# Two RMSNorm statistics moved from matmuls to GpSimd and a round trip through memory

## The chip, the cores and the metric

One core of a Trainium2 chip runs the whole program in one launch. The metric is the device time in microseconds (us) of that launch; of several runs the median is given. The core has a matrix engine (PE, TensorE, with a separate loader PEld for the stationary operand), a vector engine (DVE), an activation engine (ACT), a general engine (POOL, GpSimd) and an engine that only issues transfers (SP). On-chip memory has 128 lanes; a matmul sums over the lanes and writes to an accumulator bank, which DVE and ACT read. Each engine works off its own instructions in the order written, and waits on semaphores for those of others.

## The reference

The input is one sequence of 1024 positions with 1024 features, in float32. Two layers follow each other; each is a token mixer and a feed-forward block (FFN), both with a residual and an RMSNorm ahead. Layer 0 mixes with a short gated convolution, layer 1 with dilated attention in three branches.

```python
def rms_norm(x, g):
    y = x * lax.rsqrt(jnp.mean(x * x, axis=-1, keepdims=True) + EPS)
    return y * g

def short_conv_mixer(h, w_in, conv_k, w_out):
    b, c, u = jnp.split(h @ w_in, 3, axis=-1)
    y = depthwise_causal_conv(c * u, conv_k)          # 3 taps
    return (b * y) @ w_out

for i in range(DEPTH):                                # DEPTH = 2
    h = rms_norm(x, mix_norm[i])
    x = x + (short_conv_mixer(h, ...) if i % 2 == 0 else dilated_attention_mixer(h, ...))
    h = rms_norm(x, ffn_norm[i])
    x = x + (silu(h @ w_gate) * (h @ w_up)) @ w_down
return rms_norm(x, final_norm)
```

There are five norms: one ahead of each of the two mixers, one ahead of each of the two FFNs, and the final one. The change concerns the two ahead of the mixers.

## The kernel before

**Tiles.** Activations are kept transposed: the residual is eight tiles X of 128 features (lanes) by 1024 positions. So a sum over features, which a norm needs for each position, is a sum over the eight tiles and then over the 128 lanes. Every float32 product is made from three matmuls of a faster format: both operands are split into a high part (a copy rounded by ACT) and a low part (the difference, by DVE), and high x high, high x low and low x high are added in the bank. For weights the split is L142 (ACT) and L143 (DVE), and the weights come in by SP's loads (`load_raw`, L156, tile `raw`); sums of weights are made by DVE at L190 (tile `combo`).

**Products.** The large products are cut by Strassen's and Winograd's scheme into seven smaller products for each unit u; class `Strassen` has them in one list of pairs (u, m), and `mm` (L561 to L563) issues the three matmuls for each of four stationary tiles. After each product L567 (ACT) or L571 (DVE) takes the bank away. A list position n stands for time in this code: `start(n)` is called ahead of the n-th product, and a table of hooks says what is issued right after a certain product. So the order of work on each engine is written out by hand; nothing else decides it. The class `Conv` (layer 0) and its subclass `QueryKey` (layer 1, queries and keys) are such products. The list begins, by n: 0 (0,1), 1 (1,1), 2 (0,2), 3 (1,2), 4 (2,1), 5 (2,2), 6 (3,1), ..., 10 (0,6), 12 (0,7), 17 (1,4), 18 (2,6), 19 (0,3), 22 (2,5).

**The norm.** The products do not wait for the norm. The gain is put on the operand (L871 and L872 in the convolution; L903, L906, L907, L553, L554 for the operands that are differences), and 1/rms, which is one number for each position, is put on the results, much later: in the convolution at L969 and L959, in `QueryKey` at L1129 and L1131, and on the value tiles at L1508. Two forms are wanted: `rstd`, 128 x 1024, the same number in each lane, and `r`, 128 x 8, one number for each position in a lane. `Norm.stats` (L464 to L488) makes both from `acc`, the 128 x 1024 sum of squares over the eight tiles: eight matmuls with a column of ones sum over the lanes and leave the 1024 sums as 128 x 8 (L471, 16 instructions in the profile); ACT takes the square root (L474) and DVE the reciprocal (L475), which is `r`; DVE multiplies it with an identity into two diagonal tiles (L480); two matmuls of ones with these spread it over the lanes (L487, 4 instructions), and ACT copies the bank to `rstd` (L488). The convolution then squares `rstd` into `acc` (L1097).

In the convolution the squares (ACT, L885) are added up by accumulating transfers on GpSimd's queue (L886) into two tiles: `acc` for tiles 0 to 3, `upper` (named acc2 in the trace) for tiles 4 to 7. DVE adds the two at n = 18 (L1087); the sums over the lanes follow after product (0,3), n = 19, and the spreading after (2,5), n = 22. In `QueryKey` DVE adds the squares as each tile of X is finished (L424), the sums follow after (1,2), n = 3, and the spreading after (3,1), n = 6. The FFN norms use the same `Norm.stats`.

**Buffers and queues.** Tiles of 128 x 1024 come from a pool of 41 pages, and halves of them; a page is free when the last instruction that reads or writes it is done, so that an instruction can wait for a page that another tile had. SP's queue issues the weight loads, GpSimd's queue the stores, the accumulating transfers and the small round trips of the attention. There the attention already reduces over the lanes on GpSimd (`partition_all_reduce`, maximum, L1614) and inverts its denominators by way of memory (L1665 store, L1668 thin load, L1670 reciprocal, L1671 store, L1674 load to all lanes).

Of the kernel before, what the change touches and what calls it, by code (L numbers as in the profile page):

```python
# [98 lines left out]
def trunk(ctx: ExitStack, tc: tile.TileContext, x, gains_in, cwi, ck, cwo, wqkv, wo, relb,  # L99
# [295 lines left out]
    class Norm:  # L395
# [38 lines left out]
        def chained(self, k, c0, c1, late):  # L434


            s = slice(c0, c1)
            if self.acc is None:
                self.acc, self.rstd = page("acc"), page("rstd")
            acc = self.acc[:, s]  # L440
            if k == 1:
                self.odd = half_page("acc2")
            to = half_page("sq") if k > 1 else self.odd if k else acc
            nc.scalar.activation(to, X[k][:, s], AF.Square)
            add = lambda t: nc.vector.tensor_tensor(out=acc, in0=acc, in1=t, op=ALU.add)
            if k in (2, 3):
                nc.gpsimd.dma_start(out=(acc, self.odd)[k % 2], in_=to, accum_op=ALU.add)
            if k > 3:
                self.flush()
                self.put_off = lambda: add(to)  # L450
            if k == KT - 2:
                add(self.odd)
                self.odd = None
            if not late or k < 4:
                return
            if k == 4:
                self.rest, self.put_off = to, None
            elif k < KT - 1:
                add = lambda t: nc.vector.tensor_tensor(out=self.rest, in0=self.rest, in1=t, op=ALU.add)
            else:  # L460
                add(self.rest)
                self.rest = None

        def stats(self, c0, c1):  # L464

# [393 lines left out]
    class Conv(Strassen):  # L859
# [182 lines left out]
        def mix(self, group1):  # L1042
            norm = self.norm
            prep = self.operands()
            stats = norm.stats(0, S)

            def start(n):
                if n == 0:
# [27 lines left out]
                    next(prep)  # L1076
                elif n in (10, 12):
                    next(prep)
                elif n == 11:
                    next(prep)  # L1080
                    self.first(3)
# [1 line left out]
                    self.first(4)  # L1083
                elif n == 14:
                    next(prep, None)
                elif n == 18:
                    nc.vector.tensor_tensor(out=norm.acc, in0=norm.acc, in1=self.upper, op=ALU.add)  # L1087
                    del self.upper
                elif n == 20:
                    self.ahead = 3  # L1090

            def gather():
                next(stats)

            def spread():
                run(stats)
                nc.scalar.activation(norm.acc, norm.rstd, AF.Square)  # L1097
                self.ready = True

# [1 line left out]
            ensure(self.at(0, 1))  # L1101
            next(prep)
            ensure(self.at(0, 2))
            self.run(start, {(0, 3): gather, (2, 5): spread})
            group1("co", self.plain, self.hid)


# [3 lines left out]
    class QueryKey(Conv):  # L1111
# [43 lines left out]
        def mix(self):  # L1155
            norm = self.norm
            prep = self.differences()
            stats = norm.stats(0, S)
            x12 = []

            def start(n):
# [8 lines left out]
                elif n == 4:  # L1170
                    self.first(1)
                    ensure(self.at(4, 2))
                elif n == 5:
                    ensure(self.at(0, 6))
                elif n == 6:
                    ensure(self.at(1, 6))
# [8 lines left out]
                elif n in (10, 12):  # L1185
                    next(prep)
                elif n == 11:
                    next(prep)
                    self.first(3)
                elif n == 13:  # L1190
# [2 lines left out]
                    next(prep, None)  # L1193
                elif n == 20:
                    self.ahead = 3

            def gather():
                next(stats)

            def spread():  # L1200
                run(stats)
                self.ready = True

            def load():
                for k in range(4):
# [9 lines left out]
                start(n)  # L1215
                self.idle(n)

            norm.flush()
            self.base = op_state[1]
            ensure(self.at(0, 2))  # L1220
            self.products(filled, {(1, 2): gather, (3, 1): spread, (5, 1): load, (5, 7): last_operand})
            self.h = [[self.b[1 + 7 * h * (k < 4) + (1 + h) * (k > 3)][k % 4] for k in range(KT)] for h in range(2)]
            self.step(len(self.waiting) + 1)

# [844 lines left out]
```

## Time and profile before

| what | value |
|---|---|
| runs | 2140.90, 2142.98, 2143.33 us; median 2142.98 |
| profiled execution | 2143.59 us, its span 2141.5 us |
| PE busy | 2108.1 us (98% of the span) |
| DVE busy | 1744.0 us (81%) |
| ACT busy | 1007.4 us (47%) |
| POOL busy | 254.2 us (12%) |
| memory traffic | 212.48 MB read, 83.05 MB written, mean 138 GB/s |

How to read it: times are in us from the start of the span. A row of a timeline gives the start, the duration, the engine, the line of the kernel, the operation and its tiles (out<-in, shapes, number of instructions), and in brackets how long the engine had been idle before it and what ended that idle time. A row of the chain of waits gives start, duration and the instruction to which the end of the run is traced back. Matmuls overlap, so the row of one shows 0.39 us where they come 0.23 us apart. A line with "min/median/max" gives durations, or the time from a transfer's issue to its landing.

### The profile page before, as it was taken

Reading aid. Unit: us, or ns where it says so; the run is one execution under the profiler, and the core shown is the slowest. Engines: PE = TensorE matmul, PEld = TensorE weight load, DVE = VectorE, ACT = ScalarE, POOL = GpSimd, SP = SyncE. Lnnn points to the kernel's source line nnn. Section 1 sums busy time; section 2 is a strip of 40 time slices with the busy share of each in tenths; the row PEclk is TensorE's granted clock in tenths of the full one; section 3 lists DMA queues with packets and bytes.
Section 4 is the critical chain, followed back from the end, with each engine's and each line's share of the span. In section 5 each row is a group of like instructions: output and inputs, shape, how many; then the busy total and the mean of one; then the engine's idle time right before and its main releaser. Section 6 shows DMA issues by size and latency. Waiting matters only on the chain.

```text
span 2141.5 us, 31004 instructions
## 1 busy us (share of the span) xinstructions
PE 2108.1 (98%) x11086; PEld 1807.9 (84%) x11086; DVE 1744.0 (81%) x3272; ACT 1007.4 (47%) x1848; POOL 254.2 (12%) x370
## 2 busy tenths in 40 slices
PE   9999999999999999999999999899999999999998
PEld 7788878888888888877899989888788888888887
DVE  8798769988888888868967687777998888888876
ACT  7333426444444564335545544545543434356435
POOL 1000000110101000000323333221010101001000
PEclk9999999999999999999999999999999999999999
DMA  7322642233332576340767678755223333368432
GB/s 218 93 94 69 226 133 75 103 102 106 113 109 99 173 218 194 112 161 33 263 206 182 180 193 226 212 179 163 69 93 102 107 109 106 106 201 240 156 94 79
DMA packets 143354, 304.90 MB, mean 142 GB/s; under 512 B 48943, under 2 KB 55327, under 8 KB 143201
## 3 DMA queue, kind: packets, MB, share of 16 engines
q1 hardware_dynamic: 107488, 201.94, 31.3%
q0 software_dynamic: 28080, 86.29, 12.7%
q10 hardware_dynamic: 7632, 14.70, 1.8%
q8 instruction: 88, 1.44, 0.3%
q14 instruction: 66, 0.53, 0.1%
HBM read 212.48 MB, written 83.05 MB: 138 GB/s over the span
## 4 chain that ended last, share of the span: by engine, by line
PE 82%; DVE 7%; issue 3%; ACT 2%; DMA 2%; POOL 1%; SPq 0%; DVEq 0%; POOLq 0%; ACTq 0%
PE bank L563 19%; PE bank L561 19%; PE bank L562 19%; PE bank L371 4%; PE bank L372 4%; PE bank L370 4%; PE bank L653 3%; PE bank L656 3%; PE bank L655 3%; PE bank L1633 2%; POOL mb L1614 1%; PE bank L1503 1%; PE bank L1504 1%; PE bank L1505 1%; DVE w L143 1%
## 5 line engine op out<-in xcount | busy, mean ns | idle before, releaser
L563 PE MATMUL bank<-b,w 128*128 128x512 f32 x1952 | 761.7, 390 | 5.5 <-DVE w L143 5.3
L561 PE MATMUL bank<-b,w 128*128 128x512 f32 x1952 | 763.3, 391 | 2.1 <-ACT w L142 1.7
L562 PE MATMUL bank<-b,w 128*128 128x512 f32 x1952 | 761.1, 390 | 0.6 <-DVE b L872 0.6
L563 PEld LDWEIGHTS bank<-b,w 128*128 128x128 f32 x1952 | 366.8, 188 | 86.4 <-DVE w L143 10.2
L561 PEld LDWEIGHTS bank<-b,w 128*128 128x128 f32 x1952 | 367.0, 188 | 78.7 <-ACT w L142 2.8
L562 PEld LDWEIGHTS bank<-b,w 128*128 128x128 f32 x1952 | 366.9, 188 | 77.0 <-DVE b L872 1.8
L142 ACT ACTIVATE w<-combo 128x512 fp32r<-128x512 f32 (+2 forms) x488 | 249.2, 540 | 232.0 <-DVE combo L190 215.1
L143 DVE TENSOR_TENSOR w<-combo,w 128x512 fp32r<-128x512 f32 (+2 forms) x488 | 276.2, 579 | 39.4 <-ACT w L142 38.7
L567 ACT ACTIVATE part<-bank 128x512 f32<-128x512 f32 x186 | 110.7, 596 | 390.2 <-PE bank L563 388.5
L143 DVE TENSOR_TENSOR w<-raw,w 128x512 fp32r<-128x512 f32 (+2 forms) x342 | 189.5, 575 | 38.7 <-ACT w L142 38.7
L571 DVE TENSOR_TENSOR part<-part,bank 128x256 f32<-128x256 f32 (+1 forms) x366 | 170.5, 495 | 31.2 <-PE bank L563 16.7
L142 ACT ACTIVATE w<-raw 128x512 fp32r<-128x512 f32 (+2 forms) x342 | 166.7, 530 | 45.0 <-PE bank L563 12.2
L370 PE MATMUL bank<-w_hi,w 128*128 128x512 f32 (+1 forms) x400 | 153.8, 385 | 5.0 <-ACT w_hi L142 4.9
L371 PE MATMUL bank<-w_lo,w 128*128 128x512 f32 (+1 forms) x400 | 150.5, 376 | 1.2 <-DVE w_lo L143 1.2
L372 PE MATMUL bank<-w_hi,w 128*128 128x512 f32 (+1 forms) x400 | 150.1, 375 | 0.7 <-DVE w L143 0.7
L791 DVE TENSOR_TENSOR x<-x,bank 128x512 f32<-128x512 f32 x136 | 92.5, 680 | 29.1 <-PE bank L563 29.0
L492 DVE TENSOR_TENSOR x<-x,bank 128x512 f32<-128x512 f32 (+1 forms) x104 | 66.3, 642 | 59.6 <-PE bank L372 59.0
L190 DVE TENSOR_TENSOR combo<-raw 128x512 f32<-128x512 f32 (+1 forms) x172 | 111.1, 646 | 0.0
L370 PEld LDWEIGHTS bank<-w_hi,w 128*128 128x128 f32 x400 | 76.2, 191 | 18.8 <-ACT w_hi L142 5.4
L371 PEld LDWEIGHTS bank<-w_lo,w 128*128 128x128 f32 x400 | 76.0, 190 | 15.0 <-DVE w_lo L143 2.0
L372 PEld LDWEIGHTS bank<-w_hi,w 128*128 128x128 f32 x400 | 76.0, 190 | 14.5 <-DVE w L143 1.1
L554 DVE TENSOR_TENSOR b<-hin,b 128x512 fp32r<-128x512 f32 x126 | 79.4, 683 | 9.4 <-ACT b L553 9.4
(247 smaller groups left out, 3486.0 us busy)
## 6 DMA issues: line engine op xcount, KB each, us to landing
hin<-part SPq DMA_DIRECT2D x126, 256.0 KB
raw<-in_ffn_w_gate SPq DMA_DIRECT2D x44, 512.0 KB
raw<-in_ffn_w_up SPq DMA_DIRECT2D x44, 512.0 KB
part<-sum POOLq DMA_DIRECT2D x72, 256.0 KB, 2.3
raw<-in_ffn_w_down SPq DMA_DIRECT2D x48, 384.0 KB
raw<-in_attn_w_qkv SPq DMA_DIRECT2D x27, 512.0 KB
raw<-in_conv_w_in SPq DMA_DIRECT2D x24, 512.0 KB
part<-part POOLq DMA_DIRECT2D x36, 256.0 KB, 2.5
```

What stands on the lines that cost most here:

```text
L142: nc.scalar.activation(hi, src, AF.Copy)
L143: eng.tensor_tensor(out=lo, in0=src, in1=hi, op=ALU.subtract)
L190: eng.tensor_tensor(out=c, in0=a, in1=b, op=op)
L370: nc.tensor.matmul(b, whi[:, a], ahi[:, s], start=first, stop=False)
L371: nc.tensor.matmul(b, whi[:, a], alo[:, s], start=False, stop=False)
L372: nc.tensor.matmul(b, wlo[:, a], ahi[:, s], start=False, stop=last)
L561: nc.tensor.matmul(b, hi[:, a], bhi, start=start and k == 0, stop=False, skip_group_check=True)
L562: nc.tensor.matmul(b, hi[:, a], blo, start=False, stop=False, skip_group_check=True)
L563: nc.tensor.matmul(b, lo[:, a], bhi, start=False, stop=k == n - 1, skip_group_check=True)
L567: nc.scalar.activation(t, b, AF.Copy)
L571: nc.vector.tensor_tensor(out=t, in0=t, in1=b, op=ALU.add)
L791: nc.vector.tensor_tensor(out=X[n][:, half(h)], in0=X[n][:, half(h)], in1=b, op=ALU.add)
```

## The change

The statistics of the two mixer norms are made by a new generator, `Norm.aside`, in place of `Norm.stats`. It reduces `acc` over the lanes on GpSimd, which leaves the sum in every lane; lane 0 is stored to a small tile in memory and loaded back as 128 x 8; ACT takes the square root and DVE the reciprocal there; the result is stored to the same place, loaded to all 128 lanes as `rstd`, and loaded once more as `r`. The generator stops once (`yield`) between the thin load and the square root.

In the convolution the addition of the two accumulators becomes an accumulating transfer on GpSimd's queue at n = 10; the first part of `aside` is issued at n = 12, the second at n = 17; the squaring of `rstd` stays after (2,5). In `QueryKey` the first part is issued ahead of all products, the second at n = 5, and the flag `ready`, which lets results be taken away, is set at n = 11 in place of after (3,1). The code that GpSimd needs for its reductions is loaded ahead of the first of them, so that is now in the convolution and no longer in the attention. The FFN norms and the final norm are as before.

```diff
@@ -461,6 +461,23 @@
                 add(self.rest)
                 self.rest = None
 
+        def aside(self):
+
+            self.flush()
+            total, rd = page("total"), dram.tile([1, S], F32, name=f"rms{self.g}")
+            nc.gpsimd.partition_all_reduce(total, self.acc, 128, bass_isa.ReduceOp.add)
+            thin = consts.tile([128, KT], F32, name="thin", tag="thin", bufs=2)
+            rows = bass.AP(rd.tensor, rd.offset, [[KT, 128], [1, KT]])
+            nc.gpsimd.dma_start(rd, total[0:1])
+            nc.gpsimd.dma_start(thin, rows)
+            yield
+            nc.scalar.activation(thin, thin, AF.Sqrt, scale=1.0 / D, bias=eps)
+            nc.vector.reciprocal(thin, thin)
+            nc.gpsimd.dma_start(rows, thin)
+            nc.gpsimd.dma_start(self.rstd, bass.AP(rd.tensor, rd.offset, [[0, 128], [1, S]]))
+            r = self.r = consts.tile([128, KT], F32, name="r", tag="r", bufs=2)
+            nc.gpsimd.dma_start(r, bass.AP(rd.tensor, rd.offset, [[1, 128], [128, KT]]))
+
         def stats(self, c0, c1):
 
             self.flush()
@@ -1042,7 +1059,7 @@
         def mix(self, group1):
             norm = self.norm
             prep = self.operands()
-            stats = norm.stats(0, S)
+            stats = norm.aside()
 
             def start(n):
                 if n == 0:
@@ -1076,6 +1093,10 @@
                     next(prep)
                 elif n in (10, 12):
                     next(prep)
+                    if n == 10:
+                        nc.gpsimd.dma_start(out=norm.acc, in_=self.upper, accum_op=ALU.add)
+                    else:
+                        next(stats)
                 elif n == 11:
                     next(prep)
                     self.first(3)
@@ -1083,17 +1104,12 @@
                     self.first(4)
                 elif n == 14:
                     next(prep, None)
-                elif n == 18:
-                    nc.vector.tensor_tensor(out=norm.acc, in0=norm.acc, in1=self.upper, op=ALU.add)
-                    del self.upper
+                elif n == 17:
+                    run(stats)
                 elif n == 20:
                     self.ahead = 3
 
-            def gather():
-                next(stats)
-
             def spread():
-                run(stats)
                 nc.scalar.activation(norm.acc, norm.rstd, AF.Square)
                 self.ready = True
 
@@ -1101,7 +1117,7 @@
             ensure(self.at(0, 1))
             next(prep)
             ensure(self.at(0, 2))
-            self.run(start, {(0, 3): gather, (2, 5): spread})
+            self.run(start, {(2, 5): spread})
             group1("co", self.plain, self.hid)
 
 
@@ -1155,7 +1171,7 @@
         def mix(self):
             norm = self.norm
             prep = self.differences()
-            stats = norm.stats(0, S)
+            stats = norm.aside()
             x12 = []
 
             def start(n):
@@ -1171,6 +1187,7 @@
                     self.first(1)
                     ensure(self.at(4, 2))
                 elif n == 5:
+                    run(stats)
                     ensure(self.at(0, 6))
                 elif n == 6:
                     ensure(self.at(1, 6))
@@ -1185,6 +1202,7 @@
                 elif n in (10, 12):
                     next(prep)
                 elif n == 11:
+                    self.ready = True
                     next(prep)
                     self.first(3)
                 elif n == 13:
@@ -1194,13 +1212,6 @@
                 elif n == 20:
                     self.ahead = 3
 
-            def gather():
-                next(stats)
-
-            def spread():
-                run(stats)
-                self.ready = True
-
             def load():
                 for k in range(4):
                     x12.append(half_page("x12"))
@@ -1215,10 +1226,10 @@
                 start(n)
                 self.idle(n)
 
-            norm.flush()
             self.base = op_state[1]
+            next(stats)
             ensure(self.at(0, 2))
-            self.products(filled, {(1, 2): gather, (3, 1): spread, (5, 1): load, (5, 7): last_operand})
+            self.products(filled, {(5, 1): load, (5, 7): last_operand})
             self.h = [[self.b[1 + 7 * h * (k < 4) + (1 + h) * (k > 3)][k % 4] for k in range(KT)] for h in range(2)]
             self.step(len(self.waiting) + 1)
```

## The prediction

> **What bounds the kernel now.** Times below are of the one profiled execution, 2143.59 us (span 2141.5); it stands 0.61 us above the median of the runs, 2142.98, and I take the 0.61 off at the end. I read the page first: busy time, and the chain that ended last.
>
> ```profile
> PE 2108.1 (98%) x11086; PEld 1807.9 (84%) x11086; DVE 1744.0 (81%) x3272; ACT 1007.4 (47%) x1848; POOL 254.2 (12%) x370
> PE 82%; DVE 7%; issue 3%; ACT 2%; DMA 2%; POOL 1%; SPq 0%; DVEq 0%; POOLq 0%; ACTq 0%
> ```
>
> TensorE carries the time. So work taken from PE shortens the run one for one, unless PE then waits; work taken from DVE, ACT or POOL counts only where PE waits for it. Second, the chain in order of time, in the two stages that change: are the norm's own matmuls on it?
>
> ```profile
> 68.92 1.68 PE bank L471 x16
> 78.94 1.72 PE bank L487 x4
> 984.20 1.68 PE bank L471 x16
> 994.22 1.72 PE bank L487 x4
> ```
>
> All four groups are on it. The rows give start and time: the sums over the lanes and the spreading cost 3.40 us in each of the two norms, 6.80 in all.
>
> **The change part by part.**
> *Removed from PE.* Those four groups, 6.80 us. No matmul is added. The two FFN norms keep theirs.
>
> *Removed from DVE and ACT.* The addition of the two accumulators L1087, two L480 a norm, two copies L488 a norm. At zero: DVE and ACT follow PE there (rows below: ACT waits 3.70 us for PE at 66.24, DVE 2.75 for ACT at 82.42). They become idle time.
>
> *Added on GpSimd.* One all-reduce a norm and the round trip: a 4 KB store, a thin load, a thin store, a load to all lanes, a thin load of r. GpSimd's 12% leaves room; its queue holds nothing urgent beside them. What counts is whom the all-reduce disturbs and who waits for the trip. The attention stage has both already:
>
> ```profile
> L1614 POOL PARTITION_ALL_REDUCE mb<-m x16: 3180/3220/4057, 1125.0 to 1427.0; - x16
> 1299.27 3.18 POOL L1614 PARTITION_ALL_REDUCE mb<-m  x1
> 1299.88 1.78 DVE L1137 TENSOR_TENSOR kq_lo<-kq,kq_hi 128x512 fp32r<-128x512 f32 x1 [0.70 <-ACT kq_hi L1134]
> 1240.82 0.68 DVE L1137 TENSOR_TENSOR kq_lo<-kq,kq_hi 128x512 fp32r<-128x512 f32 x1
> 1236.80 3.22 POOL L1614 PARTITION_ALL_REDUCE mb<-m  x1 [5.32 <-issue]
> 1237.43 3.47 DVE L143 TENSOR_TENSOR w_lo<-raw,w_hi 128x1024 fp32r<-128x1024 f32 x2
> ```
>
> The same L1137 takes 0.68 us alone and 1.78 when it begins 0.61 after an all-reduce: without the hold it would have begun at 1299.88 + 1.78 - 0.68 = 1300.98, 1.71 after the all-reduce. The pair of L143 beside the other all-reduce takes 3.47, where a pair without a hold takes 2 x 1.2 (L424 of the same size: 1.23, below). So DVE, with two operands in memory, stands still until 1.7 us into an all-reduce.
> The Trainium skill's page "SBUF — State Buffer", section "Who interferes with whom", says that a DVE instruction with two SBUF inputs contends with a GpSimd instruction that reads SBUF, and that the second to issue is blocked for the whole instruction. The trace agrees on who is held, but not on how long: 1.7 of 3.2 us; the page's length is a rival below.
>
> *The hold in the attention norm.* The last addition to acc ends at 976.17, so the all-reduce begins near 976.4, beside this:
>
> ```profile
> 974.94 1.23 DVE L424 TENSOR_TENSOR acc<-acc,sq 128x1024 f32<-128x1024 f32 x1
> 976.08 0.68 DVE L143 TENSOR_TENSOR w<-raw,w 128x512 fp32r<-128x512 f32 x1
> 976.69 0.74 DVE L906 SCALAR_TENSOR_TENSOR t<-x,gains,t 128x512 f32<-128x512 f32 x1
> ...
> 978.91 0.75 DVE L907 SCALAR_TENSOR_TENSOR t<-x,gains,t 128x512 f32<-128x512 f32 x1
> 979.70 0.63 ACT L553 ACTIVATE b<-t 128x512 fp32r<-128x512 f32 x1 [0.82 <-DVE t L907]
> 980.24 1.66 ACT L142 ACTIVATE w<-raw 128x512 fp32r<-128x512 f32 x3
> 980.90 0.50 PE L561 MATMUL bank<-b,w 128*128 128x512 f32 x1 [0.63 <-ACT w L142]
> 990.47 0.62 ACT L142 ACTIVATE w<-raw 128x512 fp32r<-128x512 f32 x1
> ```
>
> DVE runs without a gap from L424 to the last L907, ACT's L553 waits for that, L142 stands behind L553, and PE waits for L142, already 0.63 us. L906 reads two operands from memory. Started at 976.4 the all-reduce holds it until 978.1, 1.4 later than now; if L143, which is running, delays the all-reduce first, until 978.5, 1.8 later. I take the middle, 1.65, all of it on PE's path. A loss of nothing (the all-reduce later than this chain) is the other end.
>
> *The trip in the attention norm.* From 976.4: 3.2 for the reduction, 3.1 for the store and 2.8 to 6.0 for the thin load (rows below) give 985.5 to 988.7; the square root now stands behind L142 of 990.47. At zero; were it later, that L142's successors would wait, and PE for them, one for one.
>
> *The convolution: the accumulator first.* The two accumulators are added by a DMA in place of DVE. It goes behind the six accumulations of L886:
>
> ```profile
> DMA to landing us min/median/max: 4.5/4.9/5.6
> 48.03 31.26 SPq L156 DMA_DIRECT2D raw<-in_conv_w_in  x7
> 49.28 2.56 ACT L871 ACTIVATE b<-x,gains 128x512 fp32r<-128x512 f32 x4
> 53.00 2.73 DVE L872 SCALAR_TENSOR_TENSOR b<-x,gains,b 128x512 fp32r<-128x512 f32 x4
> 58.12 0.69 DVE L190 TENSOR_TENSOR combo<-combo,raw 128x512 f32<-128x512 f32 x1 [1.79 <-DMA raw<-in_conv_w_in]
> 59.46 0.79 PE L563 MATMUL bank<-b,w 128*128 128x512 f32 x1 [2.35 <-DVE w L143]
> 60.05 0.63 PE L561 MATMUL bank<-b,w 128*128 128x512 f32 x1
> ...
> 62.84 0.39 PE L562 MATMUL bank<-b,w 128*128 128x512 f32 x1
> 63.07 0.39 PE L563 MATMUL bank<-b,w 128*128 128x512 f32 x1
> ```
>
> The first raw load of SP at 48.03 waited for the last accumulation (it took its page), so that landed by then. The new one issues there and lands 4.5 to 5.6 later, 52.5 to 53.6; the raw load that is now free to go some 5 us earlier shares the DMA engines, and I allow 55. The page of the second accumulator is now taken by one of the four operands made at 49.28 by ACT L871, so the last three of these, and the L872 of DVE behind them, start at 53 to 55 rather than follow on. Three L871 at 0.64, then one L872, two L190 and one L143 at 0.69: PE's operand comes at 55 + 1.9 + 4 x 0.69 = 59.7 at the late end, against 59.41 now; at the early end DVE's 1.79 us wait for the raw load hides it. The all-reduce then falls on the same DVE instructions and holds them 1.7: early it is hidden by the 1.79, late it adds all. Between a loss of nothing and 2.4 us I take 1.2.
>
> *The convolution: the trip.* GpSimd's code for the reduction is now loaded here; before the first attention reduction, where it was loaded until now, GpSimd sat idle for 6.34 us, so that is the most it can take:
>
> ```profile
> 1124.99 3.22 POOL L1614 PARTITION_ALL_REDUCE mb<-m  x1 [6.34 <-DMA ka<-kq]
> 1172.05 0.56 POOL L1665 DMA_DIRECT2D zdram<-z  x1 [5.17 <-ACT z L1656]
> 1175.16 0.59 POOL L1668 DMA_DIRECT2D zc<-zdram  x1 [2.55 <-DMA zdram<-z]
> DMA to landing us min/median/max: 2.8/5.9/6.3
> DMA to landing us min/median/max: 2.8/6.0/7.1
> 66.24 0.60 ACT L567 ACTIVATE part<-bank 128x512 f32<-128x512 f32 x1 [3.70 <-PE bank L563]
> 82.42 0.69 DVE L969 TENSOR_TENSOR part<-part,acc 128x512 f32<-128x512 f32 x1 [2.75 <-ACT acc L1097]
> ```
>
> The load starts behind the accumulation's issue, near 49, and is done by 55.3, beside the landing. So the reduction begins at 53.3 to 55.3 and ends at 56.5 to 58.5; the store takes 3.1 up to the next issue (1172.05 to 1175.16); the thin load 2.8 to 6.0 (the second landing row, L1668; the first is the store's, L1665; the thin load alone at 1175.16 is one of the short ones, with nothing ahead of it on its queue, as here). The square root ends at 62.7 to 68.0. ACT now meets it before a weight's L142, and L567 at 66.24 is behind that: with the 1.2 us of these two, PE, which would go on at 68.92, is late if the square root ends past 67.7. I take nothing, with 0.3 to 5 us kept for the range.
> The Trainium skill's "GPSIMD Engine Reference", section "2.1 Instruction dispatch", prices the first call of a freshly loaded kernel at about 6 us; the trace's bound agrees, and the sum would be the same by it.
> The load to 128 lanes (512 KB, so by the accumulations' rows some 5.6 us) goes out behind the thin store near 68 and lands near 74 to 76; ACT squares it for the DVE instruction at 82.42, some 4 us earlier after the change. At zero.
>
> *The sum.* 6.80 - 1.65 - 1.2 = 3.95 gained: 2143.59 - 3.95 = 2139.64, less 0.61: **2139.0**.
>
> **Rivals.**
> 1. *Full gain, no hold on PE's path:* 2143.59 - 6.80 - 0.61 = 2136.2. For it: in the convolution DVE has 1.79 us to give, and the order on GpSimd could put the reduction late. Against: in the attention norm nothing stands between acc and the reduction.
> 2. *The longer wait also slows PE.* PE's wait at 980.90 would grow from 0.63 to 2.28. After the 2.35 us wait at 59.46 eight matmuls took until 62.84, 3.38 us, where the next came 0.23 us on (63.07): 8 x 0.23 is 1.84, so 1.5 was lost to slower matmuls. After a shorter wait there is none:
>
> ```profile
> 1308.62 0.38 PE L1560 MATMUL bank<-qa,ka 128*128 128x256 f32 x1 [1.60 <-ACT o L1657]
> 1308.84 0.28 PE L1561 MATMUL bank<-ql,ka 128*128 128x256 f32 x1
> ```
>
> 2.28 lies nearer to 2.35 than to 1.60, but the bound between is not shown. Time: 2139.0 + 1.5 = 2140.5.
> 3. *DVE is held for the whole reduction.* L906 would wait to 979.6, 3.0 late rather than 1.65, and the convolution up to 1.5 more: 2139.0 + 1.35 + 1.5 = 2141.9, and 2143.4 with slower matmuls. Against it: the two L1137 above. This is the length by the rule of "SBUF — State Buffer" in the Trainium skill.
> 4. *The convolution's square root is a little late:* both landings at their usual 5.9 and 6.0 end it near 70.8, 3.1 past 67.7: 2142.1.
> 5. *Slower: the convolution's trip sets the time.* The code load begins only when the accumulation has landed: 55.0 + 6.3 + 4.06 (the longest reduction) + 5.9 + 7.1 + 0.3 = 78.7, PE idle for 11.0: 2150.0. It decides (2147.3, 0.2% above) from a square root at 76.0. Against it: the load waits for nothing itself.
>
> **How the numbers follow.** A measurement of this kernel tells a difference from none at about 0.2%, 4.3 us: 2138.7 and 2147.3. Chances: forecast 0.37, rival one 0.20, two 0.18, three 0.05, four 0.10, five 0.10. The forecast's own spread (the holds 1.4 to 1.8 and 0 to 2.4) is 2137.6 to 2140.4 and crosses 2138.7 about in its middle: half of it is faster. Faster 0.20 + 0.19, rounded 0.40; slower 0.10; the same 0.50. The range must hold one to four: 2135.8 (rival one less a little) to 2143.8 (rival three with slow matmuls).
>
> **What would show it.** Right: no L471 or L487 in the two stages; in the attention norm an L906 (or L907) of about 2.4 us beside the all-reduce, and the wait before the matmul near 981 grown to about 2.3; in the convolution a square root that ends before 67.7 and no PE wait behind it. Rival two shows as matmuls about 0.4 us apart after 982; rival one as L906 still 0.74; four and five as a PE wait for ACT near 69. The prediction is wrong if the reduction or the code load takes other times than in the attention stage, or if PE's wait near 59.5 moves by more than 2.4.

## The result, and the profile after

The changed kernel takes 2150.15 us (median of six runs, 2147.53 to 2154.48), the kernel before 2141.15 in the six runs now known (2137.71 to 2143.33). The ratio is 1.0047, with a 95% interval of 1.0036 to 1.0058: about 9 us slower. (Ratios here and below are formed over all runs of both kernels, so they differ by up to 0.0006 from the quotient of the two medians.) The forecast was 2139.0, in a range of 2135.8 to 2143.8.

The profiled execution of the changed kernel has a span of 2147.6 us, 6.1 more than that of before. So two traces account for 6.1 of the 9; the rest is how these executions lie to their medians, that of before, with 2143.59, 2.4 above it, that of after 0.4 below. The page after has the same shape as that of before; its first lines are busy time, share of the span and instructions of each engine:

```profile
PE 2102.4 (98%) x11046; PEld 1803.4 (84%) x11046; DVE 1747.0 (81%) x3267; ACT 1005.6 (47%) x1844; POOL 274.1 (13%) x383
```

PE works 5.7 us less than the 2108.1 of before and is done later, so it waits more. The groups by line give those waits as the last part of a row. The three matmuls of a product are L561 to L563 before and L578 to L580 after; first two rows of before, then the same two of after:

```profile
L563 PE MATMUL bank<-b,w 128*128 128x512 f32 x1952 | 761.7, 390 | 5.5 <-DVE w L143 5.3
L561 PE MATMUL bank<-b,w 128*128 128x512 f32 x1952 | 763.3, 391 | 2.1 <-ACT w L142 1.7
L578 PE MATMUL bank<-b,w 128*128 128x512 f32 x1952 | 764.4, 392 | 10.0 <-ACT w L142 9.4
L580 PE MATMUL bank<-b,w 128*128 128x512 f32 x1952 | 762.9, 391 | 8.4 <-DVE w L143 8.2
```

PE waited 7.6 us ahead of these two lines before, and waits 18.4 now. A timeline of PE shows where; these are the rows after, with the wait in brackets:

```profile
53.41 0.50 PE L578 MATMUL bank<-b,w 128*128 128x512 f32 x1 [1.77 <-ACT w L142]
60.50 0.50 PE L578 MATMUL bank<-b,w 128*128 128x512 f32 x1 [1.08 <-ACT w L142]
66.52 0.80 PE L580 MATMUL bank<-b,w 128*128 128x512 f32 x1 [5.28 <-DVE w L143]
988.17 0.80 PE L578 MATMUL bank<-b,w 128*128 128x512 f32 x1 [4.91 <-ACT w L142]
```

Three waits in the convolution stand where one of 2.35 stood, and the one of 0.63 in the attention norm has become 4.91. Behind the two long ones the matmuls come slowly, with the granted clock (the third number from the end in a row by windows: busy time and count of each engine, clock, share of the DMA engines, GB/s) at 0.87 and 0.82, where the same stretches of before have 0.93 and 1.00. The first and third row are of before, the second and fourth of after:

```profile
59.00:84.00 25.00, 24.54 (x106) 19.72 (x107) 15.95 (x26) 10.46 (x17) 0.00 (x0) 0.93 0.29 85
66.00:91.00 25.00, 24.48 (x95) 20.00 (x96) 16.69 (x28) 9.82 (x16) 2.59 (x4) 0.87 0.35 108
981.00:998.00 17.00, 17.00 (x78) 13.33 (x79) 15.84 (x26) 10.24 (x19) 0.00 (x0) 1.00 0.00 1
988.00:1005.00 17.00, 16.83 (x62) 13.60 (x63) 15.71 (x26) 10.47 (x20) 2.46 (x4) 0.82 0.07 19
```

What held the engines is seen on GpSimd and DVE, here in timelines of the two; the last row gives the three L889 one by one (min/median/max in ns):

```profile
53.26 0.84 POOL L1097 DMA_DIRECT2D acc<-acc  x1 [8.15 <-DMA acc<-sq]
58.14 6.11 POOL L468 PARTITION_ALL_REDUCE total<-acc  x1 [4.04 <-DMA acc<-acc]
979.25 6.48 POOL L468 PARTITION_ALL_REDUCE total<-acc  x1 [26.13 <-DVE acc L424]
58.74 5.79 DVE L889 SCALAR_TENSOR_TENSOR b<-x,gains,b 128x512 fp32r<-128x512 f32 x3 [2.20 <-ACT b L888]
979.67 5.03 DVE L923 SCALAR_TENSOR_TENSOR t<-x,gains,t 128x512 f32<-128x512 f32 x1
L889 DVE SCALAR_TENSOR_TENSOR b<-x,gains,b x3: 739/740/4470, 58.7 to 63.8; 128x512 fp32r<-128x512 f32 x3
```

The reductions take 6.11 and 6.48 us, not the 3.22 of those in the attention. The one L923 beside the second takes 5.03 us, where the same instruction, L906 of before, took 0.74: 4.3 lost. The three L889 beside the first take 5.79 instead of some 2.05: 3.7 lost, all of it by one of them. The other two take 0.74 as ever, though they begin before the reduction ends at 64.25. So DVE is held and then let go, and not slowed for the whole length.

Set against each other matmul by matmul, the two traces give this balance (times of after; delay of a matmul after against before, and what it grew or fell by):

| at | delay | step |
|---|---|---|
| 25 us, ahead of the change | 0.76 | |
| 53.41, behind the first wait | 2.69 | +1.93 |
| 60.50, behind the second | 4.00 | +1.31 |
| 66.52, behind the third | 7.06 | +3.06 |
| 72.23, slow matmuls | 8.23 | +1.17 |
| 77.21, no L471 | 6.74 | -1.49 |
| 85.59, no L487 | 4.87 | -1.87 |
| 949.75, ahead of the attention norm | 3.02 | -1.85 |
| 988.17, behind the wait of 4.91 | 7.27 | +4.25 |
| 993.03, slow matmuls | 9.22 | +1.95 |
| 993.45, no L471 | 7.71 | -1.51 |
| 1002.25, no L487 | 6.25 | -1.46 |
| end of the span | 6.1 | -0.15 |

The matmuls taken off PE did pay, with 6.33 us of the 6.80. In the convolution 7.47 us were lost against them, in the attention norm 6.20, so that the stages come out 4.1 and 3.2 slower. (The 1.85 between the norms is mostly a stretch of slow matmuls near 943 in the trace of before, which a second trace of that kernel does not have.)

The balance sets one execution against one, and executions differ. PE's wait near 59, 2.35 in the trace of before, is 0.47 to 2.65 in the eight other traces that have the convolution's code of before up to there. In the three of them with 0.47, 1.12 and 1.66 no slow matmuls follow, and from 25 to 77 us PE takes 2.2 to 2.6 us less than in the trace of before. Against such an execution the convolution would have lost more than 7.47. The traces also differ by several us, either way, between 1084 and 1519 in the attention, where no statistics are made. So the stages' 7.3 us are shown with their causes; how the 9 us of the medians split up is not.

### The profile page after: what moved, and what is told of

It reads as the page before. It is cut to its first block, busy times and chain, and to the rows that moved or that the text cites. A ratio compares the mean times of both kernels' runs of the same rounds, so it can differ in the third digit from the quotient of the medians.

```text
span 2147.6 us, 30928 instructions
## 1 busy us (share of the span) xinstructions
PE 2102.4 (98%) x11046; PEld 1803.4 (84%) x11046; DVE 1747.0 (81%) x3267; ACT 1005.6 (47%) x1844; POOL 274.1 (13%) x383
## 5 line engine op out<-in xcount | busy, mean ns | idle before, releaser
L578 PE MATMUL bank<-b,w 128*128 128x512 f32 x1952 | 764.4, 392 | 10.0 <-ACT w L142 9.4
L580 PE MATMUL bank<-b,w 128*128 128x512 f32 x1952 | 762.9, 391 | 8.4 <-DVE w L143 8.2
L580 PEld LDWEIGHTS bank<-b,w 128*128 128x128 f32 x1952 | 367.7, 188 | 89.8 <-DVE w L143 12.9
L578 PEld LDWEIGHTS bank<-b,w 128*128 128x128 f32 x1952 | 368.0, 189 | 87.6 <-ACT w L142 11.1
L143 DVE TENSOR_TENSOR w<-combo,w 128x512 fp32r<-128x512 f32 (+2 forms) x488 | 276.3, 579 | 44.7 <-ACT w L142 44.0
L143 DVE TENSOR_TENSOR w<-raw,w 128x512 fp32r<-128x512 f32 (+2 forms) x342 | 189.6, 575 | 38.3 <-ACT w L142 38.3
```

The lines of the kernel that those rows point to most:

```text
L143: eng.tensor_tensor(out=lo, in0=src, in1=hi, op=ALU.subtract)
L578: nc.tensor.matmul(b, hi[:, a], bhi, start=start and k == 0, stop=False, skip_group_check=True)
L580: nc.tensor.matmul(b, lo[:, a], bhi, start=False, stop=k == n - 1, skip_group_check=True)
```

## The experiments

Ratios are to the kernel before on the same chip in the same session, with 95% intervals; their medians of before are 2139.0 to 2139.7.

**The attention norm alone.** The convolution is that of before.

```diff
 class Conv: mix
-            stats = norm.aside()
+            stats = norm.stats(0, S)
...
-            self.run(start, {(2, 5): spread})
+            self.run(start, {(0, 3): gather, (2, 5): spread})
```

> Only the attention norm goes by GpSimd and memory; the convolution is as before. Theory one (the reduction with add holds DVE for over 4 us, PE waits and then runs slow matmuls for some 4 us): 3.4 us taken off PE, 4.3 of wait and 1.9 of slow matmuls added, so 2.8 us slower than before (2 to 4), with an L923 of about 5 us beside the reduction and a PE wait of about 4.9. Theory two (the loss sits in the convolution): 3 us faster than before, and that wait stays near 0.6.

Measured: 2144.79 us, ratio 1.0030 (1.0018 to 1.0042), 5.2 over the 2139.62 of before. The DVE instruction beside the reduction and PE's wait behind it:

```profile
977.25 5.03 DVE L923 SCALAR_TENSOR_TENSOR t<-x,gains,t 128x512 f32<-128x512 f32 x1
985.75 0.79 PE L578 MATMUL bank<-b,w 128*128 128x512 f32 x1 [4.91 <-ACT w L142]
```

Both are those of the full change. Theory two, that the loss sits in the convolution, is out for this part. The median is above the 2 to 4 that theory one expected, whose upper end the interval just touches (1.0018 is 3.9 us).

**The convolution alone.** The attention norm is that of before.

```diff
 class QueryKey: mix
-            stats = norm.aside()
+            stats = norm.stats(0, S)
...
-            next(stats)
+            norm.flush()
...
-            self.products(filled, {(5, 1): load, (5, 7): last_operand})
+            self.products(filled, {(1, 2): gather, (3, 1): spread, (5, 1): load, (5, 7): last_operand})
```

> Only the convolution's norm goes by GpSimd and memory; the attention norm is as before. Theory one: three PE waits (a page that comes free later, the accumulating transfer, DVE held by the reduction) cost 7.5 us in all with the slow matmuls after them, 3.4 are taken off: 4.1 slower than before (3 to 5.5). Theory two (nearly the whole loss of 9 us by the medians is here): 7 to 9 slower.

Measured: 2149.33 us, ratio 1.0044 (1.0032 to 1.0056). Its trace has the three waits of the full change within 0.11 us (1.66, 1.16 and 5.29), and the same balance: 7.4 lost, 3.5 gained. By the median it loses 9.7, more than theory one's 3 to 5.5 and even a little more than theory two had, which counted the whole loss here. Both halves are slower, and in the stages of their traces they add up to the whole (4.0 here and 3.3 in the attention norm, against 4.1 and 3.2); by their ratios they come to more than the whole, 0.74% against 0.47%. What makes that difference no run shows.

**The reduction by itself.** The kernel before, with nothing else than one reduction more.

```diff
             norm.flush()
+            nc.gpsimd.partition_all_reduce(page("total"), norm.acc, 128, bass_isa.ReduceOp.add)
             self.base = op_state[1]
```

> The kernel before, with one more reduction with add of the attention norm's accumulator into a scrap tile, at the place where the changed kernel has it; the matmuls and all else stay. Measures the disputed cost alone. Theory one: 6.2 us slower than before (5 to 7), with DVE's instruction beside the reduction at about 5 us. If the loss in the attention norm came from the trip through memory or the other moves: no difference (below 1 us).

Measured: 2144.06 us, ratio 1.0023 (1.0014 to 1.0032), so 4.4 us over before's median, a little under the 5 to 7; its trace shows 6.3 between the norm's first matmul and its last. The engines show what was expected:

```profile
972.43 6.49 POOL L1219 PARTITION_ALL_REDUCE total<-acc  x1 [26.12 <-DVE acc L424]
972.86 5.03 DVE L906 SCALAR_TENSOR_TENSOR t<-x,gains,t 128x512 f32<-128x512 f32 x1
```

A reduction whose result nobody reads holds DVE as the changed kernel's does. Neither the trip through memory nor the moved hooks are needed for the loss in the attention norm.

**Maximum in place of the sum.**

```diff
-            nc.gpsimd.partition_all_reduce(total, self.acc, 128, bass_isa.ReduceOp.add)
+            nc.gpsimd.partition_all_reduce(total, self.acc, 128, bass_isa.ReduceOp.max)
```

> The changed kernel with the maximum in place of the sum in both reductions over the lanes; nothing else differs, so the norms of the two mixers are not the reference's (the 1/rms comes from the largest lane). Theory one (DVE is held because the reduction with add takes 6.1 to 6.5 us, twice as long as the one with maximum in the attention stage): the reductions take 3.2, DVE is held 1.7 and not 4.6, PE's wait in the attention norm is 2.3 and not 4.9, the third wait of the convolution 2.5 and not 5.3: some 6 us faster than the changed kernel, 1 to 4 slower than before. If the reduction is long because DVE disturbs it and not by its operation: 6 us again, and as slow as the changed kernel.

Measured: 2143.03 us, ratio 1.0017 (1.0008 to 1.0026): 3.4 us over its before, where the changed kernel was 9.0 over. The reductions, DVE's instruction and PE's waits in the places of the full change:

```profile
58.52 3.22 POOL L468 PARTITION_ALL_REDUCE total<-acc  x1 [4.04 <-DMA acc<-acc]
976.85 3.59 POOL L468 PARTITION_ALL_REDUCE total<-acc  x1 [26.13 <-DVE acc L424]
977.27 2.38 DVE L923 SCALAR_TENSOR_TENSOR t<-x,gains,t 128x512 f32<-128x512 f32 x1
64.26 0.79 PE L580 MATMUL bank<-b,w 128*128 128x512 f32 x1 [2.64 <-DVE w L143]
983.12 0.50 PE L578 MATMUL bank<-b,w 128*128 128x512 f32 x1 [2.27 <-ACT w L142]
```

Same place, same data, same neighbours, another operation: 3.22 and 3.59 us instead of 6.11 and 6.48. So the length is that of the sum, and not made by DVE. L923 is held 1.64 us and PE waits 2.27.

**The reduction later.** The attention norm alone again, with the last addition and the reduction after product (0,2). (The code issues `start(n)` right behind the n-th product, not ahead of it as the section on the kernel has it; so n = 2 stands behind (0,2), and n = 8 behind (4,1).)

```diff
                 elif n == 1:
                     next(prep)
+                elif n == 2:
+                    next(stats)
...
                 elif n == 5:
-                    run(stats)
...
                 elif n == 8:
+                    run(stats)
...
-            next(stats)
             ensure(self.at(0, 2))
```

> Only the attention norm goes by GpSimd and memory, as in the run of that half alone, but the last addition to its accumulator (DVE L424) and with it the reduction come after product (0,2), the square root after (4,1). So DVE is held where its results are wanted later. Theory one: the waits of 4.9 and the slow matmuls behind it vanish, the 3.4 us off PE stay: 3.4 faster than before if the hold is hidden, 1 faster if some 2.4 of it shows up at PE near 990 to 995. If PE waits wherever the hold falls: 1 to 3 slower again.

Measured: 2144.65 us, ratio 1.0029 (1.0016 to 1.0041), 5.0 over before and as slow as with the reduction early; in its trace the stage loses 2.9 where it lost 3.3. The wait has moved with the hold:

```profile
985.40 5.99 DVE L143 TENSOR_TENSOR w<-raw,w 128x512 fp32r<-128x512 f32 x3
990.24 0.50 PE L580 MATMUL bank<-b,w 128*128 128x512 f32 x1 [4.08 <-DVE w L143]
```

Three L143 take 5.99 us where they took 1.89, and PE waits 4.08. In this stage DVE leads PE by too little to hide a hold of 4.1, here as there.

**DVE adds the accumulators.** The convolution alone, without the accumulating transfer.

```diff
                     if n == 10:
-                        nc.gpsimd.dma_start(out=norm.acc, in_=self.upper, accum_op=ALU.add)
+                        nc.vector.tensor_tensor(out=norm.acc, in0=norm.acc, in1=self.upper, op=ALU.add)
```

> Only the convolution's norm goes by GpSimd and memory, with one thing undone: DVE adds the two accumulators (at n = 10) in place of the accumulating transfer. If that transfer is a third of the convolution's loss (it ends at 57.9, and ACT and the reduction wait for it): the wait of 1.1 before PE's matmul at 60.5 vanishes, the reduction begins near 54 and DVE is held earlier; against the half with the transfer 3 to 5 us less, so 0 to 2 slower than before. If only the hold counts, wherever it begins: within 1 us of the half with the transfer.

Measured: 2156.9 us, ratio 1.0078 (1.0066 to 1.0090), which neither reading expected. DVE works in order, and at n = 10 the accumulations it needs have not landed:

```profile
53.06 1.23 DVE L1097 TENSOR_TENSOR acc<-acc,acc 128x1024 f32<-128x1024 f32 x1 [8.15 <-DMA acc<-sq]
54.80 7.01 DVE L946 SCALAR_TENSOR_TENSOR t<-x,gains,t 128x512 f32<-128x512 f32 x4
```

DVE stands 8.15 us behind them with all of PE's next operands queued after it, and is then held by the reduction. The run says nothing on the transfer's share; it shows why the addition was not on DVE at that place.

**The pages.** The convolution alone, with the sum written onto its own accumulator, so that no page `total` is taken.

```diff
-            total, rd = page("total"), dram.tile([1, S], F32, name=f"rms{self.g}")
+            total, rd = self.acc, dram.tile([1, S], F32, name=f"rms{self.g}")
```

> The half with only the convolution's norm changed, with one thing different: the reduction writes onto its own accumulator in place of a new page, so that the pages after it fall as before (the weight's L142 near 47 no longer waits for the last accumulating transfer, and SP's raw load does again). If the first of the three waits is the page: PE's wait of 1.7 near 53 vanishes, the last transfer lands near 48 and not 52.6, and all that follows comes some 4 us earlier; the waits for the second transfer and for the held DVE stay. 2 to 4 us faster than that half, 2 to 7 slower than before. If the wait near 53 comes from the accumulations being slow by themselves: the wait stays and the time is that of the half.

Measured: 2145.13 us, ratio 1.0024 (1.0013 to 1.0034), 5.4 over before where the half with the page was 9.7 over. The waits near 53 and 60 are gone; one is left:

```profile
49.98 0.84 POOL L1097 DMA_DIRECT2D acc<-acc  x1 [4.79 <-DMA acc<-sq]
63.94 0.79 PE L580 MATMUL bank<-b,w 128*128 128x512 f32 x1 [5.09 <-DVE w L143]
```

The transfer that adds the two accumulators goes out at 49.98 instead of 53.26. So one more page in the pool, and nothing that the change computes, made the first two waits. Who took over the page of the last square is seen in the changed kernel, in rows of ACT, SP's queue and the squares' transfers:

```profile
52.73 0.63 ACT L142 ACTIVATE w<-combo 128x512 fp32r<-128x512 f32 x1 [4.11 <-DMA acc<-sq]
43.94 22.88 SPq L156 DMA_DIRECT2D raw<-in_conv_w_in  x4
DMA to landing us min/median/max: 4.6/5.2/8.4
```

A weight's split waits 4.11 for that square's transfer. The raw load that used to wait for it until 48.03 goes out at 43.94, beside it, and the longest landing is 8.4 us where it was 5.6 before and is 5.9 without the page; that the raw load slows it is argued from these landings. In its trace the convolution without the page comes out only 0.4 us slower than in the trace of before; the 5.4 of the runs are more, as with the halves.

**Keeping PE busy in the wait.** The attention norm alone, with matmuls that nobody reads ahead of the one that waits.

```diff
+                elif n == 2:
+                    w, warm = self.b[1][0][0], bank()
+                    for _ in range(16):
+                        nc.tensor.matmul(warm, w[:, :128], w, start=True, stop=True)
```

> The half with only the attention norm changed, plus 16 matmuls of 128x512 into a bank that nobody reads, right ahead of the matmul that waits 4.9 us for the held DVE: they fill 3.6 us of that wait (0.23 each) and add no time to it. If the slow matmuls after the wait (3.0 us lost there) come from the wait itself: they vanish, PE's wait is 1.2, and the time is 2 to 3 us less than that half, 0 to 4 slower than before. If the clock drops for another reason: slow matmuls again, and the time of the half.

Measured: 2142.48 us, ratio 1.0012 (1.0003 to 1.0021), 3.4 over before where that half without them was 5.2 over.

```profile
981.12 3.79 PE L1187 MATMUL bank<-b 128*128 128x512 f32 x16
986.20 0.50 PE L578 MATMUL bank<-b,w 128*128 128x512 f32 x1 [1.29 <-ACT w L142]
```

And the 17 us that follow, in a row by windows:

```profile
986.00:1003.00 17.00, 16.80 (x73) 13.62 (x74) 16.59 (x28) 10.92 (x20) 2.55 (x4) 1.00 0.08 23
```

Without those matmuls the same stretch of that half is this:

```profile
985.00:1002.00 17.00, 16.25 (x59) 13.10 (x60) 15.17 (x26) 10.40 (x20) 3.02 (x5) 0.80 0.04 10
```

The clock behind the wait is 1.00 in place of 0.80 (0.82 in the full change), and the stage loses 0.6 us against the trace of before in place of 3.3. More work on PE made this stage faster: here the slow matmuls come from the wait. The whole times agree with that, but their intervals touch, so that they alone would not settle it.

**Only the spreading by memory.** Sums stay on PE in both norms; L480, L487 and L488 are replaced.

```diff
+            if nt == KT:
+                rd = dram.tile([1, S], F32, name=f"rms{self.g}")
+                nc.gpsimd.dma_start(bass.AP(rd.tensor, rd.offset, [[1, 128], [128, KT]]), r)
+                nc.gpsimd.dma_start(self.rstd, bass.AP(rd.tensor, rd.offset, [[0, 128], [1, S]]))
+                yield
+                return
```

> The sums over the lanes stay on PE (L471) in both norms, with root and reciprocal as before; only the spreading (L480, L487, L488) is replaced by a store of r and a load to all lanes. No reduction on GpSimd. Theory one: 1.72 us off PE in each norm, nothing held: 3.4 us faster than before (2.5 to 4). If the trip through memory itself disturbs (late in the convolution, or through the DMA engines): 0 to 3 slower, with a PE or DVE wait near 82.

Measured: 2141.76 us, ratio 1.0012 (1.0004 to 1.0021). No faster, as the second reading had it. The store of single numbers goes out at 69.12 and the load behind it only at 80.12, and PE waits in the convolution:

```profile
80.12 0.56 POOL L479 DMA_DIRECT2D rstd<-rms  x1 [10.04 <-DMA rms<-r]
88.30 0.50 PE L567 MATMUL bank<-b,w 128*128 128x512 f32 x1 [3.53 <-ACT part L573]
```

**The same with a store of 32 bytes a lane**, once with every eighth column in the sums:

```diff
+                cols = view(self.acc, t, [[KT, 128]]) if nt == KT else self.acc[:, c0 + 128 * t:c0 + 128 * t + 128]
...
+                nc.gpsimd.dma_start(bass.AP(rd.tensor, rd.offset, [[KT, 128], [1, KT]]), r)
```

> As the run with the sums left on PE, but L471 takes every eighth column, so that r lies in the order of memory and its store writes 32 bytes of each lane in one piece where it wrote eight single numbers; r in the other order is loaded once more for the attention. The store that took 10 us then takes 2 to 3; in the convolution 1/rms is in all lanes near 79. Theory: the waits of 3.5 and 0.9 near 88 vanish, and 1.72 a norm is gained: 3.4 faster than before (2 to 4). If any such trip is too late in the convolution: 0 to 2 slower, with a PE wait near 88 again.

and once with the columns as before and 1/rms read with a stride in the convolution:

```diff
+                rows = [[1, 128], [128, KT]] if self.g else [[KT, 128], [1, KT]]
+                nc.gpsimd.dma_start(bass.AP(rd.tensor, rd.offset, rows), r)
...
-                nc.scalar.activation(norm.acc, norm.rstd, AF.Square)
+                nc.scalar.activation(view(norm.acc, 0, [[128, KT], [1, 128]]), view(norm.rstd, 0, [[1, KT], [KT, 128]]), AF.Square)
```

> The sums over the lanes stay on PE in both norms with their columns as before; only the spreading goes by memory. In the convolution r is stored 32 bytes a lane, so 1/rms comes back in a changed order, and ACT's squaring and DVE's L959 read it with a stride; in the attention norm r is stored number by number (10 us, with nobody waiting). Theory (matmuls taken off PE pay in full where neither DVE is held nor the trip late): no PE wait near 88, L471 at 1.7 us again, 3.4 us faster than before (2 to 4). If the trip costs by itself: no faster, with a new PE wait.

Measured: 2144.36 us, ratio 1.0024 (1.0014 to 1.0033), for the first; 2139.46 us, ratio 1.0004 (0.9995 to 1.0013), for the second. Neither gained the 2 to 4 us expected. In both the wait near 88 is gone, the load goes out 2.2 us behind the store. In the first the sums themselves became dear:

```profile
68.94 3.74 PE L472 MATMUL bank<-ones,acc 128*128 128x1 f32 x16
```

That is twice what L471 took, 1.84; over two norms it eats up the 3.4 gained, but not the 4.7 by which this run is over its before. In the second L471 is as before, and the strided reads cost DVE and ACT instead (below). It is no faster than before by its runs, though its trace has lost L487 twice; where the 3.4 went is not settled, the less as the traced execution, 2144.62, is the slowest of its eleven. In the attention's stretch from 1245 to 1417 its PE waits longer than before's (4.87 near 1311, 1.99 in the second trace of before), and other variants vary there between 1.0 and 5.8 without a pattern that the runs show. No version here beats the kernel before.

**The kernel before once more**, unchanged.

> The kernel before, once more, for a second trace of it: which stretches of slow matmuls and which of PE's longer waits belong to the kernel, and which to the execution. Every theory expects the time of before; that of the waits, those near 25, 59, 980, 1024, 1361 and 1531 come back within 0.5 us. If the stretches of slow matmuls near 59 and 943 are matters of the execution, one of them at least is absent here.

Measured: 2139.93 us, ratio 1.0001 (0.9991 to 1.0010). The waits near 25, 59, 980, 1024, 1361 and 1531 come back (1.04, 2.00, 0.64, 0.42, 5.60, 0.99), that near 1361 with 0.7 more. The slow matmuls near 59 are there again, those near 943 are not: these belong to the execution. (That the ones near 59 do so too is seen in other runs, above.)

## Why the prediction was wrong

*What bounds the kernel, and what the matmuls are worth:* right. 6.33 us of 6.80 came back at PE.

*The hold in the attention norm:* the mechanism was right and its size wrong, and this is the step that failed first. The reduction began where the prediction put it, behind the last L424; L923, which is L906 of before, was held, and ACT and PE waited behind it. But its length and its 1.7 us of hold were read from reductions with maximum, without a question whether a sum takes the same. With the maximum in this place L923 is held 1.64 and PE waits 2.27, against 1.65 and 2.28 in the prediction; with the sum the hold is 4.3. The term was 1.65 and measured 4.25.

*Rival two, the slow matmuls:* it came true on top, with 1.95, and the run that keeps PE busy shows the wait to be the cause. The forecast had left it out and given it a chance of 0.18, for a wait of 2.28; with the maximum, at 2.27, slow matmuls did follow (1.7 us).

*The convolution's 1.2:* mis-sized, it measured 7.47, from three sources. The hold (3.06 at PE) is the same error again. The slow matmuls behind it were not in the term (1.17). And the first two waits (3.24) come from pages. That the accumulating transfer keeps the second accumulator's page was seen; that one new page shifts who takes which page after it was not, and the earlier raw load was counted as a matter of sharing the DMA engines only: 55 was allowed for the landing, which came at 57.9. (All against the one trace of before, whose wait near 59 is itself among the longer ones.)

*The trip and the code load:* right, at zero. The two pool configurations go out at 53.9 while GpSimd waits for the transfer anyway, until 57.9, and the reduction begins 4.2 us behind them, so the code load took no more than that, where 6.3 had been allowed. The trip takes 6.0 us from the store to the square root (64.55 to 70.57) and PE shows no wait behind it. The square root ended past the 67.7 that the prediction had set as its limit, and cost nothing because PE was itself some 8 us late by then. With the reduction's end where it was expected, 56.5 to 58.5, and the 0.3 and 6.0 us that followed it here, the root would have been done by 64.8, an estimate. Rivals four and five did not happen; that five's time, 2150.0, is the one measured is chance.

*Rival three*, DVE held for the whole of a 3.2 us reduction, came nearer in size (3.0 of the 4.3) for a wrong reason: neither is the reduction that short nor the hold that complete. In the runs DVE goes on before the end: with L923 taking 0.74 by itself, it was held until 4.7 us into the 6.48 of the sum, and 2.1 into the 3.59 of the maximum; in the convolution, until 4.3 into 6.11. The Trainium skill's "SBUF — State Buffer" ("Who interferes with whom") calls the port pair that DVE and GpSimd share an exclusive lock, which whoever issues first has for the whole instruction (it gives that length where it speaks of DVE's two-port modes). The runs agree that it blocks, but not to the end; still that rule, with the length that the sum has, would have given some 6.1 us for the 4.3 measured, nearer than a hold of fixed 1.7.

*The chances:* slower had 0.10, and all of it on the late trip. A hold of unknown length on a path where DVE runs without a gap should have had more.

## What to carry to other kernels

Price an operation by its own kind: a row of the same instruction with another operator is a bound at best, and where such an instruction holds another engine, what counts is its length and not its share of busy time. Before moving work to GpSimd, look at which DVE instructions with two operands in memory would run beside it, and how far DVE is ahead of PE there: at none of the three places tried here by as much as 4 us. A new buffer in a rotating pool can move the waits of all that follow it, so compare who waits for which page, and not only the order of the instructions.

## What the runs showed of the hardware that was not expected

- A reduction over 128 lanes of 128x1024 float32 takes 6.1 to 6.5 us with the sum and 3.2 to 3.6 with the maximum, in the same place. A DVE instruction with two operands in memory that begins beside the sum is held until 4.3 to 4.7 us into it, and the next begin before it ends and take their usual 0.74 us.
- Behind a wait of PE the matmuls of 128x512 come every 0.43 us instead of 0.23 for some time. In the fourteen traces this followed every wait of 2.88 us and more (up to 6.83), and most of those between 1.9 and 2.8, but not 1.91 near 53 with the maximum, 1.99 near 1307 and 2.71 near 1416 in the second trace of before, 2.52 near 1248 with the strided reads, nor 2.79 near 1316 in the changed kernel. In three of the traces it also followed two short waits close together near 1172 (1.06 or 1.26, then some 0.49), which the other traces have as well without it, and near 943 it stood in some executions with no wait ahead. So the length of a wait alone does not decide it below 2.9 us. The Trainium skill's "TensorE: Matmul & The Clock Gate" ("What's actually happening") puts the drop at an idle window of about 3.4 us; the pitch agrees with the page's cold rate, but some of the waits that sufficed here are shorter.
- Strides cost where the expectations took them as free: the stationary columns at every eighth element took 3.74 us for the sixteen matmuls where the timeline of before has 1.84, and reads with a step of eight took 1.15 us for DVE's multiplication by 1/rms (0.69 before) and 2.17 for ACT's squaring (1.06 before). This is DVE's group, in the run with the strided reads (min/median/max in ns):

```profile
L967 DVE TENSOR_TENSOR y<-y,rstd x16: 1131/1148/1173, 90.6 to 253.7; 128x512 f32<-128x512 f32 x16
```

- A store of 4 KB as single numbers held up the load behind it by 9.8 to 11.0 us, one of 32 bytes a lane by 2.2 to 2.4.
